# Two ConvFFN up-projections with seven products for eight

## The chip, the cores and the metric

The kernel runs on one core of a Trainium2 chip. The metric is the device time of one execution in microseconds (us). In what follows PE is the matmul engine (TensorE) and PEld its weight loads, DVE is VectorE, ACT is ScalarE, POOL is GpSimd, and SP is the engine whose queue issues the weight loads from memory. SBUF is the on-chip memory, PSUM the eight banks of 512 fp32 words per partition into which PE writes.

## The reference

Two layers over 528 tokens (16 learned tokens and 512 of input) of width 1024. Layer 0 is a sparse attention, layer 1 a differential attention; each is followed by a gated ConvFFN, and only that is touched here:

```
def conv_ffn(h, w_up, conv_w, conv_b, w_down):
    u = h @ w_up                                      # 1024 -> 2 x 2816
    up = jnp.pad(u, ((0, 0), (CONV_W - 1, 0), (0, 0)))
    c = conv_b + sum(up[:, j:j + Tp] * conv_w[j] for j in range(CONV_W))
    gate, val = jnp.split(c, 2, axis=-1)
    return (jax.nn.silu(gate) * val) @ w_down          # 2816 -> 1024
```

## The kernel before

Activations lie transposed: features on the partitions, tokens along the free axis, in a first half of 272 tokens (`x[0]`) and a second of 256 (`x[1]`). 2816 is 22 blocks of 128, so the up-projection of a layer has 44 tiles of 128 features: 22 blocks `f`, each with a gate (e = 0) and a value (e = 1).

Every matmul is an fp32 product in three passes. A number is split into `hi`, its rounding to the type fp32r, and `lo`, the rest; a product is hi x hi, hi x lo and lo x hi. ScalarE casts the `hi` of a weight tile (L111) and VectorE subtracts for the `lo` (L113); in what follows the two together are a split. A tile of `lin` therefore is 8 slices of the 1024 inputs x 2 halves of tokens x 3 passes = 48 matmuls (L222), accumulated in one PSUM tile of the tag `sp` (two banks; there are two such tiles). `evac` then makes the convolution: ScalarE starts it out of PSUM (L1065), VectorE adds two taps, each reading PSUM (L1068, the convolution steps). After the value tile ScalarE applies SiLU, VectorE multiplies (`c`, L1074), ScalarE casts `ah`, and VectorE subtracts `al` (L1078).

`down` multiplies the activations by `w_down`. `PARTS` cuts the 22 blocks into four parts of 6, 6, 5 and 5. When a part is complete, its eight groups `dn` (one for each 128 output features) run in a row (L1105), and VectorE adds each to the residual stream `ht` (L1116). In layer 0 (FFN0) a group works on 272 + 256 tokens, in layer 1 (FFN1) on 512.

`Weights` is a pipeline of three raw buffers and a ring of three `hi`/`lo` pairs. `add` lists the tiles in the order of use; `pump`, called whenever PE's program has finished with a tile, issues loads and splits as far as buffers are free. A list scheduler then sets the final order of the instructions on each engine. Each engine works its list from the top.

Of the kernel before, what the change touches and what calls it, by code (L numbers as in the profile page):

```python
# [17 lines left out]
KC = 8  # L18
T = 528
# [47 lines left out]
class Weights:  # L67
# [4 lines left out]
    RAW = 3  # L72
    RING = 3

    def __init__(self, nc, pool, par):
        self.nc, self.pool, self.par = nc, pool, par
        self.units, self.loads, self.raw, self.out = [], [], {}, {}
        self.loaded = self.scaled = self.ready = self.taken = self.freed = 0
        self.held = 0

    def add(self, src, n=8, m=128, g=None, lo="v", fold=None):
        self.units.append((n, m, lo))
        self.loads.append((src, n, m, g, fold))

    def load(self):
        src, n, m, g, fold = self.loads[self.loaded]
        raw = self.pool.tile([128, 8, 128], F32, tag="raw", name="raw", bufs=self.RAW)
        dst = raw[:, :n, :m]
        self.nc.sync.dma_start(dst if fold is None else dst.rearrange("p (a k) c -> p a k c", a=fold), src)
# [9 lines left out]

    def split(self):  # L100
# [5 lines left out]
        hi = self.pool.tile([128, 8, 128], F32R, tag="hi", name="hi", bufs=self.RING)  # L106
        lt = self.pool.tile([128, 8, 128], F32R, tag="lo", name="lo", bufs=self.RING)
# [33 lines left out]
    def done(self):  # L141
        self.held -= 1
# [7 lines left out]
class Trunk:  # L150
# [1497 lines left out]
```

## Time and profile before

| what | value |
|---|---|
| median of 3 runs | 1386.15 us (1383.89 to 1393.39) |
| the profiled execution | 1384.77 us, span 1383.0 us |
| mean granted clock of PE in it | 0.975 |
| busy share of the span: PE, PEld | 96%, 92% |
| busy share of the span: DVE, ACT, POOL | 62%, 43%, 21% |
| matmuls | 10072 |
| DMA | 118.98 MB, 86 GB/s in the mean |

The busy shares are means over stages with different limits. PE's matmuls are pipelined: a row's length is not the time from one matmul to the next. That time is read from runs of matmuls in the chain of waits.

### The profile page before, as it was taken

How to read it: one execution, taken by the hardware profiler on the slowest of the kernel's cores; microseconds unless marked ns; L12 is line 12 of the kernel's file. 1: busy time of each engine (PE TensorE's matmuls, PEld its weight loads, DVE VectorE, ACT ScalarE, POOL GpSimd, SP SyncE). 2: the span in 40 equal slices, each digit the busy share in tenths (PEclk: the TensorE clock that was granted, in tenths of full speed). 3: DMA queues.
4: the chain of work that ended last, by engine and by line, in shares of the span. 5: the costliest groups of instructions: out<-in, count | busy, mean ns of one | idle time of the engine just before them, and what ended most of it. 6: DMA issues, size and time to landing. Idle time of an engine off the chain costs nothing.

```text
span 1383.0 us, 25034 instructions
## 1 busy us (share of the span) xinstructions
PE 1324.3 (96%) x10072; PEld 1278.4 (92%) x10072; DVE 852.2 (62%) x1734; ACT 589.3 (43%) x1114; POOL 286.2 (21%) x334
## 2 busy tenths in 40 slices
PE   5999899999999999999799999989899999999998
PEld 4999789899999999999799999989799899899897
DVE  6499977665445445555756767775755445545453
ACT  4453555554224333234435555655544234333231
POOL 3514533400000000002554533444500000000000
PEclk9999989999999999999999989999999999999999
DMA  7412222122332232323223222212222332332422
GB/s 233 118 48 89 84 70 80 61 78 81 88 95 82 85 107 69 106 83 89 73 80 85 79 66 64 72 48 69 77 62 84 93 109 85 88 107 64 121 71 97
DMA packets 46995, 118.98 MB, mean 86 GB/s; under 512 B 5936, under 2 KB 15456, under 8 KB 46880
## 3 DMA queue, kind: packets, MB, share of 16 engines
q1 hardware_dynamic: 46128, 114.57, 27.8%
q0 software_dynamic: 752, 2.82, 0.7%
q8 instruction: 79, 1.29, 0.4%
q14 instruction: 36, 0.29, 0.1%
HBM read 112.46 MB, written 4.91 MB: 85 GB/s over the span
## 4 chain that ended last, share of the span: by engine, by line
PE 84%; DVE 8%; ACT 2%; issue 2%; POOL 2%; DMA 1%; SPq 0%; POOLq 0%; DVEq 0%; ACTq 0%
PE lin L222 56%; PE dn L1105 17%; PE pv L1005 1%; PE stq L567 1%; PE pv L1453 1%; DVE lo L113 1%; PE sa L910 1%; DVE acc L447 1%; ACT hi L111 1%; PE linh L222 1%; DVE xl L517 1%; PE pt L1014 1%; PE stk L557 1%; PE pt L1467 1%; PE sb L1379 1%
## 5 line engine op out<-in xcount | busy, mean ns | idle before, releaser
L222 PE MATMUL lin<-xh,hi 128*128 128x256 f32 (+3 forms) x2208 | 635.0, 289 | 12.7 <-DVE ht L434 7.0
L222 PE MATMUL lin<-xl,hi 128*128 128x256 f32 (+3 forms) x2208 | 634.1, 287 | 2.4 <-POOL xl L517 1.8
L222 PE MATMUL lin<-xh,lo 128*128 128x256 f32 (+3 forms) x2208 | 634.5, 288 | 0.0
L222 PEld LDWEIGHTS lin<-xh,hi 128*128 128x128 f32 (+1 forms) x2208 | 420.6, 191 | 16.3 <-ACT xh L542 5.0
L222 PEld LDWEIGHTS lin<-xl,hi 128*128 128x128 f32 (+1 forms) x2208 | 421.5, 191 | 4.3 <-POOL xl L517 2.2
L222 PEld LDWEIGHTS lin<-xh,lo 128*128 128x128 f32 (+1 forms) x2208 | 421.6, 191 | 0.1
L111 ACT CAST hi<-raw 128x1024 fp32r<-128x1024 f32 (+3 forms) x209 | 199.4, 956 | 332.3 <-PE lin L222 167.0
L113 DVE TENSOR_TENSOR lo<-raw,hi 128x1024 fp32r<-128x1024 f32 (+3 forms) x180 | 201.9, 1123 | 223.1 <-ACT hi L111 222.7
L1105 PE MATMUL dn<-ah,hi 128*128 128x256 f32 (+2 forms) x528 | 142.3, 322 | 0.5 <-DVE ht L1116 0.5
L1105 PE MATMUL dn<-al,hi 128*128 128x256 f32 (+2 forms) x528 | 142.5, 321 | 0.0
L1105 PE MATMUL dn<-ah,lo 128*128 128x256 f32 (+2 forms) x528 | 141.9, 321 | 0.0
L1068 DVE SCALAR_TENSOR_TENSOR c<-lin,par,c 128x512 f32<-128x512 f32 (+2 forms) x172 | 129.7, 755 | 2.9
L1116 DVE TENSOR_TENSOR ht<-dn,ht 128x256 f32<-128x256 f32 (+2 forms) x96 | 46.6, 514 | 116.3 <-PE dn L1105 116.3
L1105 PEld LDWEIGHTS dn<-ah,hi 128*128 128x128 f32 x528 | 88.9, 188 | 9.0 <-DVE ht L1116 0.8
L1105 PEld LDWEIGHTS dn<-ah,lo 128*128 128x128 f32 x528 | 88.9, 188 | 7.8
L1105 PEld LDWEIGHTS dn<-al,hi 128*128 128x128 f32 x528 | 89.0, 188 | 7.4
L447 POOL TENSOR_TENSOR acc<-acc,nsq 128x256 f32<-128x256 f32 (+2 forms) x18 | 16.6, 929 | 378.2 <-PE dn L1105 360.7
L113 POOL TENSOR_TENSOR lo<-raw,hi 128x1024 fp32r<-128x1024 f32 (+1 forms) x31 | 70.3, 2268 | 64.7 <-ACT hi L111 64.3
L1077 ACT CAST ah<-c 128x528 fp32r<-128x528 f32 (+1 forms) x44 | 27.6, 627 | 102.9 <-DVE c L1074 102.9
L1065 ACT ACTIVATE c<-lin,par 128x528 f32<-128x528 f32 (+1 forms) x86 | 67.2, 781 | 0.0
L1073 ACT ACTIVATE c<-c 128x528 f32<-128x528 f32 (+1 forms) x44 | 28.1, 639 | 83.7 <-DVE c L1068 83.7
L97 POOL TENSOR_TENSOR raw<-raw,par 128x1024 f32<-128x1024 f32 x24 | 47.3, 1971 | 69.1 <-DMA raw<-w_kv 34.7
(255 smaller groups left out, 1760.8 us busy)
## 6 DMA issues: line engine op xcount, KB each, us to landing
raw<-w_up SPq DMA_DIRECT2D x88, 512.0 KB, 3.5
raw<-w_down SPq DMA_DIRECT2D x32, 384.0 KB, 3.1
raw<-w_down SPq DMA_DIRECT2D x32, 320.0 KB, 2.9
raw<-w_in SPq DMA_DIRECT2D x16, 512.0 KB, 3.6
raw<-w_kv SPq DMA_DIRECT2D x16, 512.0 KB, 3.7
nb<-nbias SPq DMA_DIRECT2D x16, 264.0 KB, 2.7
raw<-w_o_a SPq DMA_DIRECT2D x8, 512.0 KB, 3.6
raw<-w_q SPq DMA_DIRECT2D x8, 512.0 KB, 3.5
```

What stands on the lines that cost most here:

```text
L97: self.nc.gpsimd.tensor_tensor(r, r, self.par[:, g:g + n, None].to_broadcast([128, n, m]), op=OP.mult)
L111: nc.scalar.copy(hi[:, :n, :m], r)
L113: eng.tensor_tensor(lt[:, :n, :m], r, hi[:, :n, :m].bitcast(F32), op=OP.subtract)
L222: i = self.nc.tensor.matmul(o, w[wi][:, kw + k, :m], x[s][xi][:, kx + k, c0:HN[s]], start=(first and p == 0), stop=(last and p == 2))
L447: eng.tensor_tensor(acc, acc, sq[:, :n], op=OP.add)
L517: i = eng.tensor_tensor(xl[:, m, o:o + n], xfs[m][:, :n], xh[:, m, o:o + n].bitcast(F32), op=OP.subtract)
L1065: nc.scalar.activation(t[:, :n], u[:, off + t0:off + T], AF.Identity, bias=b, scale=w2)
L1068: nc.vector.scalar_tensor_tensor(t[:, z:n], u[:, off + t0 + z - d:off + T - d], w, t[:, z:n], op0=OP.mult, op1=OP.add)
L1073: nc.scalar.activation(c[:, :n], c[:, :n], AF.Silu)
L1077: nc.scalar.copy(ah[:, :n], c[:, :n])
L1105: nc.tensor.matmul(part(t, c0, c1, o), w[wi][:, k, :], acts[f][ai][:, c0:c1], start=(first and p == 0), stop=(last and p == 2))
L1116: nc.vector.tensor_tensor(hv, part(t, c0, c1, o), hv, op=OP.add)
```

## The change

In each layer the blocks f = 3 to 21 are computed as pairs. The inputs of gate and value weights are cut in halves of four slices (G1, G2 and V1, V2), the tokens in two equal halves of N = 264 (FFN0) or 258 (FFN1). In place of eight products of a quarter (2 weights x 2 input halves x 2 token halves), `up_pair` makes seven, each of 4 slices x 3 passes = 12 matmuls. In the order of the program, for tiles `g` and `v` of two banks each (`g0`, `v0` the first token half, `g1`, `v1` the second):

1. g0 = G1 x (first inputs, first tokens); ScalarE copies g0 into v0, the seed.
2. g1 = S12[0:4] x T0; ScalarE copies g1 to `p5` in SBUF.
3. v0 += S12[4:8] x T1; VectorE writes g1 = v0 + p5 into PSUM (L1254).
4. g0 += G2 x (second inputs, first tokens).
5. v0 += S34[0:4] x T2; VectorE writes v1 = v0 + p5 into PSUM (L1264).
6. g1 += S34[4:8] x (second inputs, second tokens); `evac` of the gate (VectorE's steps at L1288).
7. v0 += V2 x T3; `evac` of the value.

S12 and S34 are sums of the raw weight halves: four VectorE operations of 128x512 for a pair (L176 to L181), made one pair ahead. They are split as the weights are. T0 to T3 are sums of the activations, made once a layer by GpSimd and VectorE and split by ScalarE and VectorE. Splits of the sums are all on VectorE. There are four raw buffers and a ring of five in place of three and three; a raw buffer of a gate or value is free only when both sums and its own split have read it.

The down groups have four parts of four blocks and a tail of six. The first four parts are dealt out: pair f runs one group after product 2 (its first half) and product 4 (its second), and one after products 6 and 7; the order of PE below shows where the scheduler put them. Their adds to `ht` are on VectorE as before (L1338). Only the tail's eight groups stand in a row at the end.

```diff
-    RAW = 3
...
     RING = 3
+    MORE = {"l": 1, "u": 2}
...
+    def home(self, kind, i, more):
+        near, far = self.homes[kind]
+        k = self.MORE[kind]
+        if more and self.turn[kind] >= self.RING:
+            far.append(i)
+            self.turn[kind] = (self.turn[kind] + 1) % (self.RING + k)
+            return "x", far[-1 - k] if len(far) > k else None
+        self.turn[kind] = (self.turn[kind] + 1) % (self.RING + k) if more else 0
+        near.append(i)
+        return "w", near[-1 - self.RING] if len(near) > self.RING else None
...
+    def can_load(self):
+        if self.loaded == len(self.loads):
+            return False
+        where, before = self.loads[self.loaded]["home"]
+        if where == "x" and self.extra is None:
+            return False
+        return before is None or (before < self.loaded and self.loads[before]["reads"] == 0)
...
+    def sum(self):
+        assert self.can_sum()
+        p, half = divmod(self.summed, 2)
+        p = self.pairs[p]
+        g, v = self.raw[p["g"]], self.raw[p["v"]]
+        kind = ("S12", "S34")[half]
+        t = self.extra.tile([128, 8, 128], F32, tag=kind, name=kind, bufs=1)
+        add = self.nc.vector.tensor_tensor
+        if half == 0:
+            add(t[:, 0:4], v[:, 0:4], v[:, 4:8], op=OP.add)
+            add(t[:, 4:8], t[:, 0:4], g[:, 0:4], op=OP.subtract)
+            self.s2 = t[:, 4:8]
+        else:
+            add(t[:, 4:8], g[:, 4:8], self.s2, op=OP.subtract)
+            add(t[:, 0:4], g[:, 0:4], v[:, 0:4], op=OP.subtract)
+        for r in (p["g"], p["v"]):
+            self.read(r)
+        self.sums[kind] = t
+        self.summed += 1
...
+    def can_split(self):
+        if self.ready == len(self.units):
+            return False
+        u = self.units[self.ready]
+        where, before = u["home"]
+        if (where == "x" and self.extra is None) or (before is not None and before >= self.finished):
+            return False
+        if u["kind"] == "raw":
+            return u["r"] < self.scaled
+        return self.summed > 2 * u["r"] + 1
...
-        n, m, lo = self.units[self.ready]
-        raw = self.raw.pop(self.ready)
-        self.freed += 1
-        r = raw[:, :n, :m]
...
+        u = self.units[self.ready]
+        kind, k, n, m, lo = (u[z] for z in ("kind", "k", "n", "m", "lo"))
+        src = self.raw[u["r"]] if kind == "raw" else self.sums.pop(kind)
+        r = src[:, k:k + n, :m]
...
-    PARTS = ((0, 6), (6, 12), (12, 17), (17, 22))
-    PW = ((0,0),(0,1),(1,0))
+    PLAIN = 3
+    PARTS = ((0, 4), (4, 8), (8, 12), (12, 16))
+    TAIL = 16
...
+    def down_slots(self):
+        late = {f1 + q: (p, 2 * q) for p, (_, f1) in enumerate(self.PARTS) for q in range(4)}
+        return late, {f + 1: (p, m + 1) for f, (p, m) in late.items()}
     def plan_ffn(self, l):
+        wt = self.wt
         wu, wd = self.a["w_up"][l], self.a["w_down"][l]
-        for f in range(NF):
+        wd2 = wd.rearrange("(a m) p k c -> a p m k c", m=2)
+        late, mid = self.down_slots()
+        for f in range(self.PLAIN):
             for e in range(2):
-                self.wt.add(wu[f + NF * e], lo=('p' if (f, e) in self.PW else 'v'))
-            for f0, f1 in self.PARTS:
-                if f == (f1 if f1 < NF else NF - 1):
-                    for m in range(KC):
-                        self.wt.add(wd[m][:, f0:f1, :], n=f1 - f0, lo="vv"[m % 2])
+                wt.add(wu[f + NF * e], lo='p' if (f, e) in self.PW else 'v', more=True)
+        loads = {}
+        for f in range(self.PLAIN, NF):
+            g, v = (wt.load_of(wu[f + NF * e], more=True) for e in range(2))
+            if f in late:
+                p, m = late[f]
+                f0, f1 = self.PARTS[p]
+                loads[p, m] = loads[p, m + 1] = wt.load_of(wd2[m // 2][:, :, f0:f1, :], fold=2, more=True)
+            wt.unit("raw", g, more=True)
+            pair = wt.pair(g, v)
+            wt.unit("S12", pair, more=True)
+            if f in mid:
+                wt.unit("raw", loads[mid[f]], 4, 4, more=True)
+            wt.unit("S34", pair, more=True)
+            if f in late:
+                wt.unit("raw", loads[late[f]], 0, 4, more=True)
+            wt.unit("raw", v, 4, 4, more=True)
+        for m in range(KC):
+            wt.add(wd[m][:, self.TAIL:NF, :], n=NF - self.TAIL, lo="v", more=True)
...
+            wt.extra = fp
+            TT = [tuple(fp.tile([128, 4, 264], F32R, name=f"T{w}{j}") for w in "hl") for j in range(4)]
...
+            def sums():
+                for z in range(2):
+                    nc.scalar.copy(x[1][2 + z][:, :, 0:8], x[0][2 + z][:, :, 264:272])
+                join(mid - 264, 8, 0)
+                for g, eng in enumerate((nc.gpsimd, nc.vector)):
+                    def sub(out, p, q):
+                        eng.tensor_tensor(out, p, q, op=OP.subtract)
+                    t = [pair_tile("t") for _ in range(4)]
+                    for kk in range(2):
+                        sub(t[0][:, kk], B[g, 0][:, kk], xf[2 * g + kk][:, :N])
+                    sub(t[1], B[g, 1], t[0])
+                    for kk in range(2):
+                        sub(t[3][:, kk], xf[4 + 2 * g + kk][:, :N], t[1][:, kk])
+                    sub(t[2], B[g, 1], B[g, 0])
+                    for j in (1, 0, 2, 3):
+                        hi, lo = (TT[j][z][:, 2 * g:2 * g + 2, :N] for z in range(2))
+                        nc.scalar.copy(hi, t[j])
+                        nc.vector.tensor_tensor(lo, t[j], hi.bitcast(F32), op=OP.subtract)
+            def product(out, w, wk, xs, xk, c0, first=True):
+                for k in range(4):
+                    for p, (wi, xi) in enumerate(((0, 0), (0, 1), (1, 0))):
+                        nc.tensor.matmul(out, w[wi][:, wk + k, :], xs[xi][:, xk + k, c0:c0 + N],
+                                         start=(first and k == 0 and p == 0), stop=(k == 3 and p == 2), skip_group_check=not first)
+                    self.pe(3 * mm_cost(N))
+                    self.poll()
...
+                x0, x1 = x[0][2:], x[1][2:]
+                off = 512 - mid
+                g = ps.tile([128, 1024], F32, tag="sp", name="g")
+                g0, g1 = g[:, off + st0:512], g[:, 512:512 + N]
+                G, S12 = wt.take(), wt.take()
+                product(g0, G, 0, x0, 0, st0)
+                v = ps.tile([128, 1024], F32, tag="sp", name="v")
+                v0, v1 = v[:, off + st0:512], v[:, 512:512 + N]
+                nc.scalar.copy(v0, g0)
+                product(g1, S12, 0, TT[0], 0, 0)
+                p5 = fp.tile([128, 264], F32, tag="p", name="p5", bufs=2)[:, :N]
+                nc.scalar.copy(p5, g1)
+                a = at_mid.get(f)
+                a = a and down(*a)
+                if a:
+                    next(a)
+                product(v0, S12, 4, TT[1], 0, 0, False)
+                nc.vector.tensor_tensor(g1, v0, p5, op=OP.add)
+                if f + 1 < NF:
+                    wt.sum()
+                product(g0, G, 4, x0, 4, st0, False)
+                wt.done()
+                wt.done()
+                if a:
+                    next(a)
+                S34 = wt.take()
+                product(v0, S34, 0, TT[2], 0, 0, False)
+                nc.vector.tensor_tensor(v1, v0, p5, op=OP.add)
+                product(g1, S34, 4, x1, 4, mid - 264, False)
+                evac(g, f, 0, off)
+                wt.done()
+                b = at_late.get(f)
+                b = b and down(*b)
+                if b:
+                    next(b)
+                if f + 1 < NF:
+                    wt.sum()
+                A22 = wt.take()
+                product(v0, A22, 0, TT[3], 0, 0, False)
+                evac(v, f, 1, off)
+                if b:
+                    next(b)
+                wt.done()
...
-            def down(f0, f1):
-                last = f1 == NF
-                squares = last and l == 0
...
+            def new():
+                cnt[0] += 1
+                if cnt[0] % 2 and cnt[0] > 40:
+                    t = ps.tile([128, 1024], F32, tag="sp", name="dn")
+                elif l == 1:
+                    t = ps.tile([128, 512], F32, tag="one", name="dn")
+                else:
+                    t = self.halves("dn")
+                return t, wt.take()
+            def down(p, m):
+                f0, f1 = self.PARTS[p]
+                t, w = new()
+                for k in range(f1 - f0):
+                    if k == (f1 - f0) // 2:
+                        yield
+                    block(t, w, f0 + k, k, cols, k == 0, k == f1 - f0 - 1)
+                add(t, m, cols, False)
+                wt.done()
+                yield
...
+            at_late, at_mid = self.down_slots()
             for f in range(1, NF):
+                if f >= self.PLAIN:
+                    up_pair(f)
+                    continue
...
                         self.run(self.lin(x, lambda u, f=f, e=e: evac(u, f, e), start=st0, tag="sp"))
-                for f0, f1 in self.PARTS[:-1]:
-                    if f == f1:
-                        down(f0, f1)
+                        if f == self.PLAIN - 1:
+                            wt.sum()
...
-            down(*self.PARTS[-1])
+            down_last(self.TAIL, NF)
```

VectorE in FFN0, before: one block f, from the split of the next gate tile to `al` (the numbers are the tiles'):

```order
L113 TENSOR_TENSOR lo_5010<-raw_4830,hi_5009 128x1024
L1068 SCALAR_TENSOR_TENSOR c0_5005<-lin_4956,par_73,c0_5005 128x527
L1068 SCALAR_TENSOR_TENSOR c0_5005<-lin_4956,par_73,c0_5005 128x526
L113 TENSOR_TENSOR lo_5075<-raw_4889,hi_5074 128x1024
L1068 SCALAR_TENSOR_TENSOR c1_5064<-lin_5015,par_73,c1_5064 128x527
L1068 SCALAR_TENSOR_TENSOR c1_5064<-lin_5015,par_73,c1_5064 128x526
L1074 TENSOR_TENSOR c0_5005<-c0_5005,c1_5064 128x528
L1078 TENSOR_TENSOR al_5071<-c0_5005,ah_5070 128x528
```

A block's eight rows are two splits, four convolution steps, `c` and `al`; nothing else stands between them.

VectorE in FFN0, after: the start of a step at pair f = 9 (`g_5002`, `v_5015`), from the add into g1 on; `lo_5184`, `lo_5196` are halves of w_down, `S12_5255` and `S34_5337` the sums for the pair f = 11.

```order
L1254 TENSOR_TENSOR g_5002<-v_5015,p5_5029 128x264
L211 TENSOR_TENSOR lo_5180<-S12_5058,hi_5179 128x1024
L211 TENSOR_TENSOR lo_5192<-S34_5140,hi_5191 128x1024
L1264 TENSOR_TENSOR v_5015<-v_5015,p5_5029 128x264
L211 TENSOR_TENSOR lo_5184<-raw_4880,hi_5183 128x512
L1288 SCALAR_TENSOR_TENSOR c0_5122<-g_5002,par_73,c0_5122 128x527
L1288 SCALAR_TENSOR_TENSOR c0_5122<-g_5002,par_73,c0_5122 128x526
L211 TENSOR_TENSOR lo_5196<-raw_5077,hi_5195 128x512
L1288 SCALAR_TENSOR_TENSOR c1_5155<-v_5015,par_73,c1_5155 128x527
L176 TENSOR_TENSOR S12_5255<-raw_5189 128x512
L181 TENSOR_TENSOR S34_5337<-raw_5187,raw_5189 128x512
L1338 TENSOR_TENSOR ht_72<-dn_5229,ht_72 128x256
```

Splits, sums, PSUM adds, convolution steps and down adds of three pairs now alternate, and the add into v1 (`v_5015`) stands behind two splits.

VectorE after, pair f = 10 (`g_5199`, `v_5212`), from its add into g1 to its add into v1:

```order
L1254 TENSOR_TENSOR g_5199<-v_5212,p5_5226 128x264
L211 TENSOR_TENSOR lo_5277<-raw_5187,hi_5276 128x1024
L1338 TENSOR_TENSOR ht_72<-dn_5426,ht_72 128x256
L1338 TENSOR_TENSOR ht_72<-dn_5425,ht_72 128x272
L211 TENSOR_TENSOR lo_5389<-S34_5337,hi_5388 128x1024
L181 TENSOR_TENSOR S34_5534<-raw_5384,raw_5386 128x512
L211 TENSOR_TENSOR lo_5377<-S12_5255,hi_5376 128x1024
L1264 TENSOR_TENSOR v_5212<-v_5212,p5_5226 128x264
```

Between the two adds stand three splits and one of the sums for f = 12, whose raw tiles `raw_5384` and `raw_5386` are loaded into buffers that earlier splits free; `raw_5386` takes the buffer of `raw_5187`, read for the last time by `lo_5277`.

PE before, at the border of two tiles of `lin`:

```order
L222 MATMUL lin_5015<-xl1_3352,hi_4885 128x256
L222 MATMUL lin_5015<-xh1_3351,lo_4886 128x256
L222 MATMUL lin_5080<-xh0_3478,hi_4950 128x272
L222 MATMUL lin_5080<-xl0_3479,hi_4950 128x272
```

The next tile follows the last at once, in the other PSUM tile.

PE after, at the border of the pairs f = 10 and f = 11: the end of product 7, four down matmuls and the start of product 1.

```order
L1225 MATMUL v_5212<-Th3_3425,hi_5270 128x264
L1225 MATMUL v_5212<-Tl3_3426,hi_5270 128x264
L1225 MATMUL v_5212<-Th3_3425,lo_5271 128x264
L1327 MATMUL dn_5521<-ah_4176,hi_5392 128x256
L1327 MATMUL dn_5520<-ah_4176,hi_5392 128x272
L1327 MATMUL dn_5521<-al_4177,hi_5392 128x256
L1327 MATMUL dn_5520<-al_4177,hi_5392 128x272
L1225 MATMUL g_5396<-xh0_3500,hi_5276 128x264
L1225 MATMUL g_5396<-xl0_3501,hi_5276 128x264
L1225 MATMUL g_5396<-xh0_3500,lo_5277 128x264
```

Now four matmuls of a down group stand between product 7 and the next product 1, which writes the PSUM tile that the gate's convolution steps read.

## Rows read from the trace of the kernel before

**Rows 1.** Two stretches: busy us (count) by engine, clock, DMA share, GB/s.
```profile
293.20:634.00 340.80, 340.80 (x2785) 340.80 (x2786) 178.25 (x239) 117.22 (x149) 0.00 (x0) 1.00 0.30 89
1023.00:1351.00 328.00, 328.00 (x2377) 310.06 (x2378) 174.48 (x215) 116.00 (x150) 0.00 (x0) 1.00 0.32 93
```

**Rows 2.** Chain that ended last, FFN0: start us, us, what, count.
```profile
293.17 64.84 PE lin L222 x528
358.01 35.26 PE dn L1105 x288
393.26 70.49 PE lin L222 x576
```

**Rows 3.** The same chain, FFN1.
```profile
1022.90 62.84 PE lin L222 x528
1085.73 33.41 PE dn L1105 x144
1119.15 68.29 PE lin L222 x576
```

**Rows 4.** VectorE, 330 to 640 us, by shape: count, busy us, mean ns, idle before.
```profile
L113 DVE TENSOR_TENSOR lo<-raw,hi 128x1024 fp32r<-128x1024 f32 x33 | 40.4, 1225 | 58.5 <-ACT hi L111 58.3
...
L1068 DVE SCALAR_TENSOR_TENSOR c<-lin,par,c 128x527 f32<-128x527 f32 x36 | 27.3, 759 | 0.0
...
L1074 DVE TENSOR_TENSOR c<-c,c 128x528 f32<-128x528 f32 x18 | 12.8, 708 | 0.6
L1078 DVE TENSOR_TENSOR al<-c,ah 128x528 fp32r<-128x528 f32 x18 | 12.7, 707 | 10.6 <-ACT ah L1077 10.6
L1116 DVE TENSOR_TENSOR ht<-dn,ht 128x272 f32<-128x272 f32 x24 | 10.3, 430 | 0.0
L1116 DVE TENSOR_TENSOR ht<-dn,ht 128x256 f32<-128x256 f32 x24 | 10.2, 424 | 49.2 <-PE dn L1105 49.2
```

**Rows 5.** VectorE, whole span, shapes of FFN1.
```profile
L1068 DVE SCALAR_TENSOR_TENSOR c<-lin,par,c 128x512 f32<-128x512 f32 x86 | 64.2, 748 | 1.4
...
L1116 DVE TENSOR_TENSOR ht<-dn,ht 128x512 f32<-128x512 f32 x32 | 22.0, 690 | 60.2 <-PE dn L1105 60.2
...
L1078 DVE TENSOR_TENSOR al<-c,ah 128x512 fp32r<-128x512 f32 x22 | 15.2, 691 | 13.3 <-ACT ah L1077 13.3
```

**Rows 6.** ScalarE, whole span, by shape.
```profile
L111 ACT CAST hi<-raw 128x1024 fp32r<-128x1024 f32 x136 | 142.4, 1047 | 193.6 <-PE lin L222 129.7 <-PE dn L1105 56.1 <-POOL tm L889 2.8
L1065 ACT ACTIVATE c<-lin,par 128x528 f32<-128x528 f32 x43 | 33.9, 787 | 0.0
...
L1077 ACT CAST ah<-c 128x512 fp32r<-128x512 f32 x22 | 13.6, 620 | 53.7 <-DVE c L1074 53.7
...
L1475 ACT COPY of<-pv 128x272 f32<-128x272 f32 x8 | 3.0, 379 | 2.6 <-PE pv L1453 2.5
```

**Rows 7.** VectorE in order of time: start us, us, engine, line, operation.
```profile
362.59 0.77 DVE L1116 TENSOR_TENSOR ht<-dn,ht 128x256 f32<-128x256 f32 x2 [0.62 <-PE dn L1105]
363.28 0.95 DVE L113 TENSOR_TENSOR lo<-raw,hi 128x768 fp32r<-128x768 f32 x1
364.14 0.70 DVE L1078 TENSOR_TENSOR al<-c,ah 128x528 fp32r<-128x528 f32 x1
```

**Rows 8.** DMA issues of the page: KB each, median us from issue to landing.
```profile
raw<-w_up SPq DMA_DIRECT2D x88, 512.0 KB, 3.5
```

**Rows 9.** Chain that ended last, start of FFN0.
```profile
291.76 0.50 issue
292.26 0.77 DVE c L1068
293.03 0.14 issue
```

**Rows 10.** Three short stretches, columns as in the first group.
```profile
288.00:293.20 5.20, 3.74 (x31) 3.55 (x29) 3.89 (x5) 4.92 (x7) 0.00 (x0) 1.00 0.30 76
664.00:670.00 6.00, 2.33 (x16) 1.63 (x15) 5.89 (x11) 2.50 (x6) 0.98 (x1) 0.85 0.34 91
670.00:676.00 6.00, 5.07 (x24) 4.56 (x24) 6.00 (x11) 2.55 (x7) 4.80 (x3) 0.58 0.24 83
```

More of the change, by code (lines that the diff above doesn't have):

```diff
@@ L67 @@
 class Weights:
-    RAW = 3
     RING = 3
+    MORE = {"l": 1, "u": 2}
     def __init__(self, nc, pool, par):
         self.nc, self.pool, self.par = nc, pool, par
[L77 to L83, printed above, removed]
-    def load(self):
[L86 to L89, printed above, removed]
+        self.loads, self.units, self.pairs = [], [], []
+        self.raw, self.out, self.sums = {}, {}, {}
+        self.loaded = self.scaled = self.summed = self.ready = self.taken = self.finished = 0
+        self.extra = None
+        self.homes = {"l": ([], []), "u": ([], [])}
+        self.turn = {"l": 0, "u": 0}
@@ new lines, in unit, with pair, add @@
+    def unit(self, kind, r, k=0, n=8, m=128, lo="v", more=False):
+        if kind == "raw":
+            self.loads[r]["reads"] += 1
+        i = len(self.units)
+        self.units.append({"kind": kind, "r": r, "k": k, "n": n, "m": m, "lo": lo, "home": self.home("u", i, more)})
+    def pair(self, g, v):
+        self.pairs.append({"g": g, "v": v})
+        for r in (g, v):
+            self.loads[r]["reads"] += 2
+        return len(self.pairs) - 1
+    def add(self, src, n=8, m=128, g=None, lo="v", fold=None, more=False):
+        self.unit("raw", self.load_of(src, n, m, g, fold, more), 0, n, m, lo, more)
@@ new lines, in place @@
+    def place(self, home, tag, dt):
+        if home == "x":
+            k = self.MORE["l" if tag == "raw" else "u"]
+            return self.extra.tile([128, 8, 128], dt, tag="x" + tag, name=tag, bufs=k)
+        return self.pool.tile([128, 8, 128], dt, tag=tag, name=tag, bufs=self.RING)
+    def can_load(self):
[5 more added lines that the diff above has]
+        return before is None or (before < self.loaded and self.loads[before]["reads"] == 0)
@@ L90, in load @@
+    def load(self):
+        d = self.loads[self.loaded]
+        raw = self.place(d["home"][0], "raw", F32)
+        dst = raw[:, :d["n"], :d["m"]]
+        f = d["fold"]
+        self.nc.sync.dma_start(dst if f is None else dst.rearrange("p (a k) c -> p a k c", a=f), d["src"])
         self.raw[self.loaded] = raw
@@ L113, in split @@
         eng.tensor_tensor(lt[:, :n, :m], r, hi[:, :n, :m].bitcast(F32), op=OP.subtract)
+        if kind == "raw":
+            self.read(u["r"])
         self.out[self.ready] = (hi, lt)
-        self.held += 1
         self.ready += 1
-    def can_split(self):
-        return self.ready < self.scaled and self.held < self.RING
     def pump(self, stop=None):
         while stop is None or self.ready < stop:
-            if self.loaded < min(len(self.loads), self.freed + self.RAW):
+            if self.can_load():
                 self.load()
@@ L141, in done @@
     def done(self):
-        self.held -= 1
+        self.finished += 1
         self.pump()
@@ L1118, in add, with down_last @@
                         self.norm_sum(fp, int(c0 == 272), m)
[L1120 to L1136 removed]
+            def new():
[17 more added lines that the diff above has]
+                yield
+            def down_last(f0, f1):
+                squares = l == 0
+                nf = f1 - f0
+                cnt[0] = 40
+                for grp in [(0, 1), (2,), (3,), (4,), (5,), (6, 7)]:
                     tw = [new() for _ in grp]
```

55 lines of the change are left out of this document (39 added, 16 removed).

## The prediction

> **What bounds the kernel now.** I read first the table of stretches, since the whole-span shares mix stages [rows 1]: from 293.2 to 634 us (the first ConvFFN, "FFN0") and from 1023 to 1351 us (FFN1) the matmul engine (PE) is busy all of the time at a granted clock of 1.00 (the level of 2.4 GHz), VectorE about half of it (178.25 of 340.8 us), ScalarE a third, GpSimd not at all. The chain of waits agrees: in both stages it is PE alone, runs of matmuls with nothing between them [rows 2, 3]. So there a matmul taken away is time won, as long as nothing else becomes the bound. The runs give the price: in FFN0 64.84/528 to 70.49/576 = 0.1224 us for a matmul of 264 columns on average; in FFN1 0.1186 us for one of 258 and 33.41/144 = 0.232 us for one of 512. Third, the groups by shape price VectorE and ScalarE [rows 4 to 6].
>
> **What it removes.** A gate/value pair takes 7 products of 4x3 matmuls in place of 96 matmuls: 84. The change does this for 19 of 22 pairs in each layer: 228 matmuls fewer in each, 228 x 0.1224 = 27.9 us and 228 x 0.1186 = 27.0 us. Together **54.9 us**, all on the path, since PE is the path. The down products keep their number of matmuls; they are dealt out, two groups to a pair, where before eight stood in a row.
>
> **What it adds, for one pair with its two down groups.** The weights are split from 3.5 pieces (G, S12, S34 and half of V) in place of two, with two halves of w_down. On VectorE in FFN0: three splits of 1024 at 1.225 and three of 512 at about 0.70 [rows 4, 5] (for a split of 512 no row stands; I take the subtraction `al` of 512, 0.691, and of 528, 0.707), 5.8 us; four sums of 512 at 0.69, 2.8; two adds into PSUM, for which the trace has no row: at least the 0.43 of an add of 272 that reads PSUM, at most the 0.76 of a convolution step twice as wide, and I take 0.43, 0.9; four convolution steps 3.05; `c` and `al` 1.4; the adds of two down groups 1.7. That is **15.6 us** against PE's 84 x 0.1224 + 48 x 0.1224 = **16.2**. In FFN1, with 0.748 for a convolution step and 0.69 for a down add [rows 5], 15.1 against 84 x 0.1186 + 24 x 0.232 = 15.5. ScalarE: three casts of 1024 at 1.047, three of 512 at 0.62, two PSUM copies at 0.38 (the copy out of PSUM of 272 columns; it writes SBUF and not PSUM, so 0.3 to 0.6 bound it), and two convolution starts, a SiLU and a cast, 2.9: 8.7 us [rows 6], far from full. DMA bytes don't change.
>
> So VectorE goes from half to about 95% busy. Its rows overlap a little: the one that starts at 363.28 lasts 0.95, and the next starts at 364.14, 0.09 early [rows 7]. With 0.08 off each row that doesn't read the one ahead, 15.6 becomes about 14.3. The Trainium skill ("VectorE: DVE Perf Modes", "The DRAIN you can't avoid") says that the next operation doesn't start until the pipeline of the last is empty, except where one is not held. The rows show the small overlap; without it a step holds 15.6 us of VectorE, which is the third rival.
>
> **What decides is the order.** VectorE, ScalarE and PE each work their list from the top, and a row that waits holds all behind it. I walk one step in FFN0 after the other along the new lists, with the durations above, 0.15 us between engines (the issue piece of 0.14 in [rows 9]) and 3.5 us from the issue of a raw load to its landing [rows 8]. Zero is the end of product 3 of pair f=9.
>
> f=9: PE does products 4 to 7 (to 5.9), 28 down matmuls, product 1 of f=10, 20 down matmuls, products 2 and 3, to 16.1. VectorE needs 16.4, of which it idles 2.7: for the cast of S12, whose buffer product 3 frees (0.65); for the cast of a down half freed by product 6 (1.0) and the convolution start behind it; for a raw load (0.75). PE loses nothing, VectorE ends 0.3 late.
>
> f=10: PE does 24 down matmuls (19.1) and products 4, 5, 6 (23.5). VectorE splits G until 18.55; only that frees the raw buffer of the load that the S34 sum needs, which lands at 22.1. The sum waits at the head of the list, behind it a split (1.15) and the add that reads v0: done 24.4. Product 7 overwrites v0, so it starts 1.0 late, ends 26.0. The four down matmuls next need a cast whose buffer product 7 has just freed: 0.95 late. Product 1 and 20 down matmuls end 31.35; product 2 waits for the seed copy of v0, which needs the second convolution step of the last v (31.0) and stands behind a cast on ScalarE: 32.4, 1.1 late. Product 3 ends at 35.4: 19.2 us for 16.2 of matmuls.
>
> f=11 in the same way ends at 52.2 (16.8 for 15.4: the S12 sum waits for a load that the split of G freed, and the down split that PE needs stands behind it), f=12 at 71.6 (19.4 for 17.4). Four steps: 71.6 us against 65.1 of matmuls, **1.6 us of waiting a step**, a little more than the 1.47 that a pair saves. In FFN1 PE's step is 0.6 us shorter and VectorE's 0.5: I take 1.8.
>
> **Starts and ends.** In the first three pairs VectorE also makes the T tiles (8 splits, 6 subtractions) and two pairs' sums; at 288 to 293 us PE already waits there for VectorE's convolution steps to free PSUM [rows 9]. Its list from the norm's last step to the first add into PSUM is some 60 rows of 0.36 to 1.15 us, by these prices 38 us, where PE has 33 us of matmuls and the 5 us of waiting that is there already; walked, the last plain tile comes 3.4 us late, since VectorE frees its PSUM late: I take **4 us** a layer (0 to 8). Three steps a layer have few or no down matmuls to cover VectorE: f=3 (12.5 us of matmuls; I estimate 15.0), f=19 (13.2; 16.4), f=20 (10.3; 13.9, where product 1 of f=21 stands directly behind product 7 and waits for g's convolution steps): **9.3 us** a layer. The down groups at the end are cover for VectorE, at no cost.
>
> **The sum.** 15 steps x 1.6 + 15 x 1.8 + 2 x 4 + 2 x 9.3 = 77.6 us of new waiting, less 54.9: +22.7 on the profiled execution's 1384.8, so 1407.5; the median of the runs is 1.4 above it, so **1408 us**, 1.6% slower. Its own range is 1394 to 1420 (a third of a microsecond a step either way).
>
> **Rivals.** *VectorE keeps up* (faster): PE stays the path, and the adds and the convolution steps are done before PE wants their banks. For it: 14.3 of 16.2 us is room enough if the idle pieces fall together, and before, PE waited nowhere. Against it: 2.7 us of idle in the mildest step. It decides where VectorE's step with its idle time stays under 16.2 (15.5) us. Price: 54.9 less 8 at the starts, 9 at the ends, 0.2 a step: -32, 1354 us (1340 to 1372). *The loads come in time*: the median of 3.5 us is that of loads issued long ahead, and if buffers free earlier than I walk, the sums never hold the list; that takes about half of the waiting in f=10 and f=11. Steps then lose 0.8 and 1.0: 27 + 26.6 - 54.9 = -1, 1385 us (1372 to 1394). *No overlap on VectorE*: 15.6 + 2.7 = 18.3 us a step and 17.8 in FFN1, 2.1 and 2.3 of waiting: 66 + 26.6 - 54.9 = +38, 1424 us (1420 to 1436). The clock is no rival of its own: at 288 to 293 us PE idles 1.5 us and keeps 1.00; only behind 664 to 670 us, where it works 2.33 of 6, does it fall (0.85, then 0.58) [rows 10], and no step here idles so much.
>
> **How the numbers follow.** Walked order 0.47, loads in time 0.27, VectorE keeps up 0.18, no overlap 0.08. The 8-in-10 range is 1352 to 1430: it cuts half of the fast case and part of the slowest. About 1% (1372 to 1400) is what this measurement can tell from no change: faster 0.18 + 0.02 = 0.20; slower, the walked case above 1400 (0.37) and the slowest (0.08), 0.45; within 1% the rest, 0.35.
>
> **What would show it.** Right: in the FFN stretches PE under 95% busy, VectorE over 85%; in the chain of waits VectorE's splits, sums and convolution steps between the products; PE's waits before product 7 put down to the add at L1264, before product 1 to L1288, before product 2 to ScalarE's copy at L1245; VectorE's sums (L176 to L181) waiting for raw loads; a step of 17.5 to 18 us in FFN0. The first matmul cut shows in the counts (about 456 fewer). Wrong: PE still full and the span near 1350, or VectorE idle over 15% while PE waits for ScalarE or loads alone.

## The result, and the profile after

The changed kernel takes 1455.8 us (median, 1452.91 to 1458.25) against 1389.8 for the kernel before in the same comparison: ratio 1.048, 95% interval 1.043 to 1.053. Forecast was 1408, range 1352 to 1430: the direction was right, the size was off by a factor of three. The spans are 1456.0 and 1383.0 us.

The stretches of the changed kernel, columns as in [rows 1]: the 19 pairs of FFN0 and of FFN1, and the start of FFN0 in pieces of 10 us.

```profile
324.04:664.20 340.16, 305.76 (x2382) 295.51 (x2381) 257.08 (x392) 152.88 (x221) 0.00 (x0) 0.99 0.27 83
1085.22:1422.14 336.92, 301.86 (x1998) 270.65 (x1996) 252.20 (x360) 152.29 (x222) 0.00 (x0) 0.98 0.28 85
290.00:300.00 10.00, 2.92 (x24) 2.70 (x22) 7.31 (x9) 6.94 (x12) 7.50 (x10) 0.81 0.00 1
300.00:310.00 10.00, 6.84 (x44) 6.87 (x45) 10.00 (x16) 4.48 (x7) 0.00 (x0) 0.68 0.34 107
310.00:320.00 10.00, 8.48 (x69) 8.30 (x68) 10.00 (x16) 4.78 (x8) 0.00 (x0) 1.00 0.04 8
```

Against [rows 1], PE is down from 100% to 90% busy in both, as forecast. But VectorE is busy 75.6% and 74.9%, not over 85%. Both engines have time to spare, so how they hand work to each other is the first suspect; the experiments below test that against VectorE's load and the raw loads. The waits view of PE, whole span (who waited for whom, us of idle time, times, longest; only the rows of the two FFNs):

```profile
PE lin L318 <- DVE c L1288: 23.4, 4, 10.2
PE g L1225 <- ACT v L1245: 22.9, 24, 2.8
PE g L1225 <- DVE g L1254: 13.3, 20, 1.1
...
PE dn L1327 <- DVE lo L211: 11.0, 10, 3.0
PE dn L1327 <- ACT hi L209: 7.9, 13, 0.7
PE v L1225 <- DVE v L1264: 6.4, 6, 1.4
```

The second and third rows are products 2 and 4. Neither needs what it waits for. Product 2 writes g1, and waits for ScalarE's copy, which reads g0; product 4 adds to g0, and waits for VectorE's add, which writes g1. g0 and g1 lie in two banks, but in one PSUM tile, and the waits go by the tile (the runs e1 and e13 below, with product 2 in a tile of its own, bear this out). The chain of waits at pair f = 9 (start, us, what) shows both:

```profile
436.30 0.37 ACT v L1245
436.67 0.04 issue
436.71 1.72 PE g L1225 x12
438.44 1.47 PE v L1225 x12
...
440.00 0.45 DVE g L1254
440.45 0.04 issue
440.49 1.72 PE g L1225 x12
```

The copy at 436.30 is late for a reason that VectorE's list in order of time shows (start, us, engine, line, operation):

```profile
433.04 0.76 DVE L1288 SCALAR_TENSOR_TENSOR c<-v,par,c 128x527 f32<-128x527 f32 x1
433.71 0.68 DVE L180 TENSOR_TENSOR S<-raw,S 128x512 f32<-128x512 f32 x1
434.31 1.22 DVE L211 TENSOR_TENSOR lo<-raw,hi 128x1024 fp32r<-128x1024 f32 x1
435.44 0.76 DVE L1288 SCALAR_TENSOR_TENSOR c<-v,par,c 128x526 f32<-128x526 f32 x1
```

The copy writes v0 of the new pair, so it needs the tile v of the pair before, and that is free only after both convolution steps have read it. Between the two stand a sum and a split, 1.7 us. In the kernel before the steps read PSUM in the same way, but the other tile of `lin` gave PE 48 matmuls, 5.9 us by [rows 2], before the first was needed again.

### The profile page after: what moved, and what is told of

Read it like the earlier page. It is cut to its first block, busy times and chain, and to the rows that moved or that the text cites. A ratio compares the mean times of both kernels' runs of the same rounds, so it can differ in the third digit from the quotient of the medians.

```text
span 1456.0 us, 24823 instructions
## 1 busy us (share of the span) xinstructions
PE 1304.9 (90%) x9616; PEld 1234.7 (85%) x9616; DVE 1071.0 (74%) x2106; ACT 687.9 (47%) x1302; POOL 316.0 (22%) x362
## 4 chain that ended last, share of the span: by engine, by line
PE 61%; DVE 21%; DMA 7%; issue 4%; ACT 4%; POOL 1%; SPq 0%; DVEq 0%; ACTq 0%; POOLq 0%
PE lin L318 21%; PE dn L1327 11%; PE g L1225 10%; PE v L1225 7%; DVE lo L211 6%; DMA raw<-w_up 6%; DVE c L1288 3%; ACT hi L209 2%; PE stq L688 1%; PE pv L1688 1%; PE pv L1126 1%; DVE ht L1338 1%; DVE xl L638 1%; PE sa L1031 1%; DVE nxf L657 1%
## 5 line engine op out<-in xcount | busy, mean ns | idle before, releaser
L318 PE MATMUL lin<-xh,hi 128*128 128x272 f32 (+4 forms) x992 | 290.7, 298 | 34.4 <-DVE c L1288 23.4
L318 PE MATMUL lin<-xl,hi 128*128 128x272 f32 (+4 forms) x992 | 291.5, 295 | 3.2 <-DVE xl L638 2.9
L209 ACT CAST hi<-raw 128x512 fp32r<-128x512 f32 (+3 forms) x225 | 185.8, 828 | 229.2 <-PE g L1225 60.0
L318 PE MATMUL lin<-xh,lo 128*128 128x272 f32 (+4 forms) x992 | 290.5, 294 | 0.0
L211 DVE TENSOR_TENSOR lo<-raw,hi 128x512 fp32r<-128x512 f32 (+3 forms) x196 | 188.3, 963 | 58.1 <-ACT hi L209 57.8
L318 PEld LDWEIGHTS lin<-xh,hi 128*128 128x128 f32 (+1 forms) x992 | 191.7, 196 | 38.1 <-ACT Th L1219 20.4
L318 PEld LDWEIGHTS lin<-xl,hi 128*128 128x128 f32 (+1 forms) x992 | 193.9, 195 | 5.2 <-DVE xl L638 4.7
L318 PEld LDWEIGHTS lin<-xh,lo 128*128 128x128 f32 (+1 forms) x992 | 193.8, 195 | 0.1
L1327 PE MATMUL dn<-ah,hi 128*128 128x272 f32 (+2 forms) x528 | 145.4, 326 | 8.0 <-ACT hi L209 7.9
L1225 PE MATMUL g<-xh,hi 128*128 128x264 f32 (+1 forms) x456 | 133.4, 293 | 20.7 <-DVE g L1254 13.3
L1327 PEld LDWEIGHTS dn<-ah,lo 128*128 128x128 f32 x528 | 90.2, 190 | 22.7 <-DVE lo L211 15.7
```

The costliest lines, as they stand in the source:

```text
L209: nc.scalar.copy(hi[:, :n, :m], r)
L318: i = self.nc.tensor.matmul(o, w[wi][:, kw + k, :m], x[s][xi][:, kx + k, c0:HN[s]], start=(first and p == 0), stop=(last and p == 2))
L1225: nc.tensor.matmul(out, w[wi][:, wk + k, :], xs[xi][:, xk + k, c0:c0 + N], start=(first and k == 0 and p == 0), stop=(k == 3 and p == 2), ...
L1327: nc.tensor.matmul(part(t, c0, c1, o), w[wi][:, k, :], acts[f][ai][:, c0:c1], start=(first and p == 0), stop=(last and p == 2))
```

## The experiments

Theory A: PE loses at hand-offs, because a PSUM tile is held by readers and a product waits for the whole tile. Theory B: VectorE's load sets the step. Theory C: the raw loads set it, through the sums that wait for them (34.3 us of VectorE's idle time in all). Ratios are to the kernel before, with 95% intervals. Line numbers shift by a few where an edit adds lines.

**Product 2 in a bank of its own** (e1):

```diff
-                product(g1, S12, 0, TT[0], 0, 0)
+                q = ps.tile([128, 512], F32, tag="one", name="q")[:, :N]
+                product(q, S12, 0, TT[0], 0, 0)
...
-                nc.scalar.copy(p5, g1)
+                nc.scalar.copy(p5, q)
```

> Product 2 writes a PSUM bank of its own instead of the second bank of tile g, so it no longer waits for ScalarE's copy of g0 into v0. In the changed kernel PE waits 26.8 us at product 2 for that copy, plus some 3 us of restarts. Theory A (uncovered hand-offs: a product waits for a reader of the other bank of its tile, and nothing covers it): 24 to 30 us less, 1426 to 1432 us. Theory B (VectorE's load sets the step) and theory C (the raw loads set it): the wait moves to another product, at most 6 us less, 1450 to 1456.

1426.1 us, 1.028 (1.025 to 1.032): 30 us less, the number that A had. (No matmul of the pair starts the sum in g1's bank any more, and the output changes with it; the instructions are as many.) PE's waits show another way to it than A's:

```profile
PE q L1225 <- ACT hi L209: 16.6, 7, 5.3
PE g L1225 <- DVE g L1255: 16.1, 20, 1.5
PE v L1225 <- ACT v L1245: 15.9, 15, 2.8
...
PE lin L318 <- DVE c L1289: 8.8, 3, 4.2
```

Product 2 (`q`) waits for the copy no more, so that wait did go by the tile. But product 3, which truly needs v0, now waits 15.9 us for the same late copy, and product 2 waits 16.6 for the cast of its weights, 10.4 of it in the first pairs, where it now stands among the plain tiles. Without these 10.4, products 2 and 3 together wait 22.1 us, against 22.9 before. What fell are the waits at the down groups (18.9 to 7.2 for casts and splits), at product 7 (6.4 to none) and at product 1, and some at the plain tiles. The match with A's range is in part luck: this run does not show that product 2's wait by itself costs 30 us.

**Sums of weights on GpSimd** (e4):

```diff
-        add = self.nc.vector.tensor_tensor
+        add = self.nc.gpsimd.tensor_tensor
```

> The four sums of weights of each pair go from VectorE to GpSimd, which is idle in the FFN stretches. VectorE loses 4 x 0.69 = 2.8 us of its 13.5 us a pair. Theory B: the step follows VectorE, 1.2 to 2.5 us less a pair, 45 to 95 us in all, 1360 to 1410 us. Theory C: the sums still wait for the raw loads but hold only GpSimd's list, 15 to 30 us less, 1425 to 1440. Theory A: under 12 us less, since VectorE is idle a quarter of the time, 1444 to 1456.

1427.3 us, 1.030 (1.026 to 1.034): 28 us less, in nobody's range but C's, and C falls with the next run. A was wrong that VectorE's list hardly matters: with four rows a pair fewer in it, PE's wait at product 7 went (6.4 us before), that at the down groups fell from 18.9 to 10.2 us and that at product 2 from 22.9 to 18.1, while that at product 4 rose from 13.3 to 17.2. B was wrong that the step follows the load. Nor did the load fall as it should: 106 us of sums left VectorE, but its busy time fell only from 1071.0 to 1046.2 us. Groups of VectorE by shape, 330 to 640 us, in the changed kernel:

```profile
L211 DVE TENSOR_TENSOR lo<-raw,hi 128x512 fp32r<-128x512 f32 x49 | 33.6, 686 | 5.7 <-ACT hi L209 5.6
...
L1288 DVE SCALAR_TENSOR_TENSOR c<-g,par,c 128x527 f32<-128x527 f32 x17 | 13.0, 762 | 0.0
...
L1294 DVE TENSOR_TENSOR c<-c,c 128x528 f32<-128x528 f32 x17 | 12.0, 705 | 0.5
```

and with the sums on GpSimd:

```profile
L211 DVE TENSOR_TENSOR lo<-raw,hi 128x512 fp32r<-128x512 f32 x50 | 44.2, 886 | 10.5 <-ACT hi L209 10.5
...
L1294 DVE TENSOR_TENSOR c<-c,c 128x528 f32<-128x528 f32 x19 | 21.2, 1114 | 0.8
...
L1288 DVE SCALAR_TENSOR_TENSOR c<-g,par,c 128x527 f32<-128x527 f32 x18 | 13.8, 764 | 3.7 <-ACT c L1285 3.6
```

Operations with two inputs in SBUF got slower (686 to 886 ns, 705 to 1114); the one that takes an input from PSUM didn't (762 to 764).

**Five raw buffers** (e6; `MORE["l"]` from 1 to 2) and **a ring of six** (e7; `MORE["u"]` from 2 to 3):

> Five raw buffers instead of four. VectorE sits idle 16.5 us in FFN0 before sums whose raw tile has not landed, and the chain of waits of the changed kernel goes through raw loads for 86 us. Theory C: 20 to 40 us less, 1415 to 1435 us. Theories A and B: under 8 us less, 1448 to 1456.

> A ring of six hi/lo buffers instead of five. PE waits some 24 us at down groups for a cast or a subtraction that got its buffer late. If the ring holds these (part of theory A: hand-offs), 12 to 22 us less, 1434 to 1444 us. Theory B: the splits are late because VectorE is busy, under 6 us less, 1450 to 1456. Theory C: under 6 us.

Five raw buffers: 1455.8 us, 1.049 (1.046 to 1.053). VectorE's waits for loads fell from 34.3 to 14.8 us and the time stayed the same: theory C is out as what sets the time. A ring of six: 1469.1, 1.061 (1.056 to 1.065), 13 us slower, which no theory had. The down groups' waits nearly went, but the seed copy's grew. ScalarE's seed copy (count, busy us, mean ns, idle before and what ended it), in the changed kernel

```profile
L1245 ACT COPY v<-g 128x264 f32<-128x264 f32 (+1 forms) x38 | 13.8, 362 | 57.1 <-DVE c L1288 44.1 <-PE g L1225 11.3 <-DVE ht L1338 1.6
```

and with the ring of six:

```profile
L1245 ACT COPY v<-g 128x264 f32<-128x264 f32 (+1 forms) x38 | 13.7, 362 | 58.9 <-DVE c L1288 57.7 <-PE g L1225 1.3
```

ScalarE idles as long before it, now almost only for VectorE's convolution steps, and PE waits at product 2 in all 38 pairs, 62.5 us against 22.9: what the ring saved at the down groups (18.9 us, now 2.3) came back there, and more. That splits which run ahead stand before the convolution steps is the likely reason for the "more"; no run takes it by itself.

**Quarters** (e8): every quarter in a PSUM tile of one bank, and ScalarE copies it to SBUF, where the convolution reads it. The down groups take the two-bank tiles. (One matmul more in the first pair of each layer opens v0's bank; 9618 matmuls in all.)

```diff
-                g = ps.tile([128, 1024], F32, tag="sp", name="g")
-                g0, g1 = g[:, off + st0:512], g[:, 512:512 + N]
+                def quarter(name):
+                    return ps.tile([128, 512], F32, tag="one", name=name)[:, :N]
+                g0, g1 = quarter("g"), quarter("g")
...
+            def evac_quarters(q0, q1, f, e):
+                u = fp.tile([128, T], F32, tag="uv", name="u", bufs=2)
+                nc.scalar.copy(u[:, st0:mid], q0)
+                nc.scalar.copy(u[:, mid:T], q1)
+                evac(u, f, e, 0)
```

> Each of g0, g1, v0, v1 is a PSUM tile of one bank, and ScalarE copies the finished quarters into SBUF, from where the convolution reads; the down groups take the tiles of two banks. No product waits for a reader of another bank any more. VectorE's work is the same, ScalarE has four copies of some 0.37 us more for a pair. Theory A: of the changed kernel's waits of PE, 27.0 us at product 2 and 16.9 us at product 4 go, and most of the 8.1 us at product 7 and of the 23.7 us at the down groups, since other matmuls can stand between: 50 to 75 us less, 1381 to 1406 us. Theory B: VectorE's 13.5 us of work in a list with its own waits still sets the step; the waits come back elsewhere, at most 30 us less, 1426 us or more.

1344.9 us, 0.970 (0.967 to 0.973): 111 us less than the changed kernel, 3% faster than the kernel before. Two stretches, and a piece of the chain, which is PE alone again:

```profile
330.00:612.00 282.00, 282.00 (x2321) 282.00 (x2320) 247.37 (x385) 167.61 (x289) 0.00 (x0) 1.00 0.32 98
1040.00:1300.00 260.00, 260.00 (x1812) 243.31 (x1812) 228.80 (x334) 156.39 (x270) 0.00 (x0) 1.00 0.34 102
```

```profile
446.01 1.47 PE g L1225 x12
447.48 1.45 PE v L1225 x12
448.93 1.45 PE g L1225 x12
450.38 2.20 PE dn L1335 x18
```

VectorE does all that it did in the changed kernel, is 88% busy, and holds nobody up in these stretches. Theory B is out for this arrangement.

**Quarters with sums on GpSimd** (e9), **with a ring of six** (e11):

> The quarters, and the sums of weights on GpSimd. Theory A: VectorE has room, and the sums' 2.8 us beside GpSimd's slowing of its SBUF operations changes little: within 10 us of the quarters alone. Theory B: 20 to 30 us less than the quarters alone, as the sums on GpSimd gave 28 without the quarters.

> The quarters, and a ring of six. In the changed kernel six gave 13 us more, because splits that ran ahead stood before the seed copy and the adds (product 2 waited 68 us). Theory A: with the quarters a late seed copy has products 2 and 4 and down matmuls to hide it, so within 8 us of the quarters alone. Theory B (the order of the lists of VectorE and ScalarE sets the step): again 10 to 20 us slower than the quarters alone.

Sums on GpSimd: 1374.5, 0.993 (0.990 to 0.995), 30 us *slower* than the quarters alone; neither theory had the sign. Now the convolution reads SBUF too. Its steps, VectorE's groups over the whole span, with the quarters alone

```profile
L1296 DVE SCALAR_TENSOR_TENSOR c<-u,par,c 128x526 f32<-128x526 f32 x39 | 29.7, 761 | 0.1
L1296 DVE SCALAR_TENSOR_TENSOR c<-u,par,c 128x527 f32<-128x527 f32 x39 | 29.7, 761 | 1.4 <-ACT c L1293 1.4
```

and with the sums on GpSimd:

```profile
L1296 DVE SCALAR_TENSOR_TENSOR c<-u,par,c 128x526 f32<-128x526 f32 x39 | 46.2, 1185 | 0.8
L1296 DVE SCALAR_TENSOR_TENSOR c<-u,par,c 128x527 f32<-128x527 f32 x39 | 43.1, 1106 | 4.8 <-ACT c L1293 4.7
```

With 2.8 us of sums a pair taken off it, VectorE is as busy as with them (249.68 us of 330 to 612, against 247.37), and its adds into g1 come late: PE waits 19.8 us for them. The ring of six: 1335.7, 0.963 (0.961 to 0.965), 9 us faster, just outside A's 8 and against B's sign: what cost 13 us while VectorE held PSUM is worth 9 when it doesn't.

**Which part of the quarters did it.** The copies alone, in one piece out of the two-bank tiles (e12):

```diff
-                evac(g, f, 0, off)
+                evac_copy(g, f, 0, off)
...
+            def evac_copy(q, f, e, off):
+                u = fp.tile([128, T], F32, tag="uv", name="u", bufs=2)
+                nc.scalar.copy(u[:, st0:T], q[:, off + st0:off + T])
+                evac(u, f, e, 0)
```

> As the changed kernel, with g and v in PSUM tiles of two banks, but ScalarE copies a finished tile into SBUF in one piece and the convolution reads that, so that VectorE's four convolution steps no longer hold PSUM. The quarters did this too, gained 111 us, and this run tells how much of it is the copy. Theory A1 (the wait for a whole tile is what costs): products 2 and 4 still wait some 0.65 to 0.75 us each, 38 pairs x 1.4 = 53 us stay: 1400 to 1430 us. Theory A2 (VectorE's convolution steps that hold the tile cost most): 70 us or more less than the changed kernel, 1385 us or less.

1390.7 us, 1.002 (1.000 to 1.005): 65 us less than the changed kernel, level with the kernel before, and between the two ranges (A1 1400 and more, A2 1385 and less). The copies give 65 of the quarters' 111 us, so VectorE's hold on PSUM is the larger part, as A2 had it, if by less. The waits at product 1 (7.3 us) are gone, those at the down groups fell from 18.9 to 2.4 us, that at product 2 halved; those at product 4 and at the plain tiles stayed. PE's waits with the copies:

```profile
PE lin L318 <- DVE c L1293: 21.9, 4, 10.3
...
PE g L1225 <- DVE g L1254: 11.8, 16, 2.3
PE g L1225 <- ACT v L1245: 11.3, 8, 2.8
```

The copies, with product 2 in its own bank in all but the first pair (e13), and the copies for the plain tiles of f = 0 to 2 too (e14):

> The copies, and product 2 in a PSUM bank of its own (all but the first pair). Left of the whole-tile waits is that of product 4 for the add into g1. Theory A1: about 25 to 30 us less than the copies alone, and 20 to 30 us (38 x 0.75, and what follows from it) above the quarters' 1345: 1365 to 1385 us. Theory A2: within 8 us of the copies alone.

> The copies alone, and also for the tiles of the first three blocks, whose PSUM VectorE's convolution steps hold while VectorE makes the T tiles. With the copies alone the first pair still starts some 14 us later than 288 matmuls after the start of FFN0 would let it. Theory S1 (the start is lost because these steps free PSUM late): the first pair starts 6 to 12 us earlier in each layer, 1368 to 1380 us against 1391 for the copies alone. Theory S2 (the T tiles and the first splits themselves are late): within 5 us of the copies alone.

e13: 1399.8, 1.007 (1.004 to 1.011), 9 us slower than e12: A1 missed this one, and A2 by 1 us. Product 2's wait for the copy is left only in the two first pairs (5.5 us, where it was 11.3), but product 2 now waits 5.1 us for the cast of its weights, product 3 for the copy 3.0, and the down groups 6.8 in place of 2.4. To free product 2 alone is worth nothing here. e14: 1380.2, 0.996 (0.994 to 0.998), 10.5 us less than e12, at the edge of S1's range: the start is held by convolution steps in part. But the first pair starts only 3.9 us earlier (321.0 for 324.9), where S1 had 6 to 12. PE's wait there went from 21.9 us for VectorE to 12.9 for ScalarE's copies:

```profile
PE lin L318 <- ACT u L1283: 12.9, 4, 4.1
```

Last, only g in two one-bank tiles, v in a two-bank tile (e16; e12's copies, piece by piece for g):

```diff
-                g = ps.tile([128, 1024], F32, tag="sp", name="g")
-                g0, g1 = g[:, off + st0:512], g[:, 512:512 + N]
+                g0, g1 = (ps.tile([128, 512], F32, tag="one", name="g")[:, :N] for _ in range(2))
```

> Copies for the convolution, and only g in two PSUM tiles of one bank; v keeps its tile of two banks, of which there are now two for the v alone. So products 2 and 4 no longer wait for readers of the other bank of g, and nothing else of the quarters is there. Theory A (the 46 us between the copies alone, 1391, and the quarters, 1345, are the whole-tile waits at products 2 and 4 and the first pair that waits for a two-bank tile): 1340 to 1360 us. Rival D (they are the down groups' tiles of two banks and v's quarters): 1375 to 1395 us.

1348.1 us, 0.972 (0.968 to 0.976): A's range, and all but 3 us of the 46 between e12 and e8. Freeing g0 from g1, and g from the two-bank tiles that the plain tiles and v use, is what the quarters add to the copies; v's quarters are not needed. Three things changed at once here: g0 is free of g1; the first pair need not wait for a two-bank tile; and v has two such tiles to itself. PE's waits at products 2 and 4 (11.3 and 11.8 us in e12) are gone. At the plain tiles they fell from 21.9 to 0.4 us, and the first pair begins at 298.9 us in place of 324.9; of that, 11.8 us came back as waits of g's products for casts and splits. How the 43 us divide between the three is not shown, and e13, which freed product 2 alone, gained nothing. Its FFN0:

```profile
330.00:612.00 282.00, 282.00 (x2319) 282.00 (x2319) 249.61 (x386) 165.60 (x270) 0.00 (x0) 1.00 0.33 100
```

One more, the quarters with a ring of six and copies for the plain tiles:

> The quarters with a ring of six, and copies for the tiles of the first three blocks too. There products of the first pair already fill PE's waits at the start, so S1 and S2 both give little: 1328 to 1338 us against 1336; the time that 54.9 us of matmuls less would give with no wait at all is 1331.

1348.9, 0.973 (0.970 to 0.977), 13 us slower than without those copies, above the expected range (part of the products' sums comes out changed in this kernel). The extra copies moved products of the first pair to other places in PE's list; why that costs 13 us was not followed up.

## Why the prediction was wrong

**What it removes** was right: 9616 matmuls against 10072, 456 fewer, and 54.9 us stays the price: a wait-free end would be 1384.8 - 54.9 = 1329.9, and the profiled execution of the quarters with a ring of six takes 1334.7.

**What it adds** was right row by row. In FFN0's pairs:

```profile
L211 DVE TENSOR_TENSOR lo<-S,hi 128x1024 fp32r<-128x1024 f32 x36 | 44.0, 1223 | 15.2 <-ACT hi L209 15.1
L211 DVE TENSOR_TENSOR lo<-raw,hi 128x512 fp32r<-128x512 f32 x50 | 34.3, 686 | 6.6 <-ACT hi L209 6.5
...
L176 DVE TENSOR_TENSOR S<-raw 128x512 f32<-128x512 f32 x17 | 11.7, 690 | 9.0 <-DMA raw<-w_up 8.9
...
L1254 DVE TENSOR_TENSOR g<-v,p 128x264 f32<-128x264 f32 x19 | 8.4, 441 | 19.9 <-PE v L1225 19.8
```

A split of 512 took 0.686 (0.70 taken), a sum 0.690 (0.69), an add into PSUM 0.441 (0.43). Rows overlap by 0.06 each (the rows of this stretch sum to 279.6 us, busy 257.08, 392 rows), so the rival without overlap is out. What failed is the share: "about 95%", and over 85% as a sign, where 75.6% and 74.9% were measured. VectorE needs 13.5 us a pair (257.08/19, edges included), and PE's waits stretched the step. With the quarters VectorE is 88% busy and PE 100%.

**What decides is the order** was the right mechanism, and the walk was close where it was made: the four steps from f = 9 to 13 took 73.0 us (end of product 3 at 439.90 to 512.90) against 71.6. PE's waits before products 7, 1 and 2 are put down to the rows named (6.4 us to L1264, 4.3 to L1288, 22.9 to L1245). The step that failed is the next one, the size of the term: these four were taken for all, 1.6 us a step in FFN0 and 1.8 in FFN1. Counted in the trace from product 3 to product 3, the 15 middle steps of FFN0 wait 35.0 us (2.3 a step), of FFN1 40.4 (2.7), where 24 and 27 were forecast. The four walked ones wait 7.9 us, not 6.5; the other eleven of FFN0 wait 27.1, 2.5 a step. The worst, from f = 7, waits 4.9 and 7.3 us, 2.1 and 3.0 of it for the split of a down half, which VectorE's list has behind other rows. The walk as told has product 2's wait only at f = 10 and that of product 4 nowhere (13.3 us over the span): it read the list for the operands each product needs, and the wait at product 4 is for none of these.

**Starts** were the second mis-sized term: 4 us a layer forecast. 144 of the 288 plain matmuls stand ahead of 293.17 us in [rows 2], so without a wait the first pair would begin at 293.17 + 144 x 0.1224 = 310.8; it begins at 324.04, 13.2 late. In FFN1 the same count gives 1022.90 + 144 x 0.1186 + 35.95 (by which its start has moved, 1000.18 to 1036.13) = 1075.9 against 1085.22, 9.3 late. The cause was named rightly ("VectorE frees its PSUM late"), and "PE lin for DVE c", 23.4 us, is its row; the walk of the last plain tile priced it at a third. "The clock is no rival" failed there too, if by little: from 300 to 310 us the granted clock is 0.68, a mean of 2.4 and 1.2 GHz, after a stretch with PE busy 2.92 of 10 us, and its 44 matmuls took 6.84 us, 1.4 more than at 0.1224. It fell inside the pairs too, where the prediction had no step idle enough for it. These are the steps from f = 13 in FFN0 and from f = 7 in FFN1, in which PE stands idle for 2.5 and 4.6 us:

```profile
512.90:533.29 20.39, 17.92 (x128) 17.07 (x127) 14.40 (x22) 8.29 (x13) 0.00 (x0) 0.92 0.35 115
1159.69:1181.80 22.11, 17.52 (x107) 15.36 (x107) 13.44 (x20) 7.65 (x12) 0.00 (x0) 0.92 0.22 71
```

At 0.92 such a step loses some 1.6 to 1.8 us (an estimate: 8% of its length), out of the 4.7 and 7.3 counted as waiting above.

**The sum.** FFN0's pairs: 1596 + 783 matmuls x 0.1224 = 291.2 of 340.16, 49.0 of waiting; FFN1's: 1596 x 0.1186 + 399 x 0.232 = 281.9 of 336.92, 55.0. With the starts 126.5, less 54.9 is +71.6; the spans differ by 73.0. Forecast were 33.3, 36.3 and 8, less 54.9: +22.7. The edges (9.3 a layer forecast, 10.2 and 10.7 measured) were nearly right; the rest, 3.8 and 3.9, lies ahead of the first product 3 and behind the last.

**The rivals.** "VectorE keeps up" had the price nearly right (1354) for a kernel that the change could have been: it needed PSUM tiles, not VectorE time. "The loads come in time" is out by e6: they nearly did, and nothing moved. The range missed because no case in it waited more than the four walked steps, but for one that hung on VectorE's speed. A case in which more of the steps wait for PSUM tiles that are held too long, with both engines idle, was not priced.

## What to carry to other kernels

When an engine's work is cut into shorter pieces, look at who still reads the buffer of the last piece and how many rows of other work stand in that reader's list between its reads; a cheap copy on an engine with time to spare (0.59 us a tile here) can be worth more than the work saved (65 us against 54.9). Ask of every wait whether the waiter needs the data or only the tile: here two banks in one tile wait for each other's readers. But look at the next product as well: where it truly needs the same late copy, to free the first alone gains nothing (e13). And before an engine's load is called the bound, see whether it idles: here moving load away gained 28 us where the convolution read PSUM and lost 30 where it read SBUF.

## What the runs showed of the hardware

GpSimd slows VectorE where both read SBUF: beside its sums, VectorE's operations with two SBUF inputs went from 705 to 1114 ns and from 761 to 1185, while the convolution step with one input in PSUM stayed at 762 to 764. The Trainium skill ("SBUF — State Buffer", "Who interferes with whom") says that a VectorE instruction with two SBUF inputs contends with a GpSimd instruction that reads SBUF, and that one with at most one SBUF input, outside the 2-port modes, doesn't; these rows agree.

In the chains, a product behind a wait takes 1.72 us for its 12 matmuls and one in a stream 1.47: a stop costs 0.25 us beyond its idle time.
